# First rows of a one-core encoder layer: where S5's exponential, the mixing weights' row sums, the row scaling and the third weights' products stand in the order of work

## The chip, the cores and the metric

The kernel runs on one core of a Trainium2 chip. Its engines work side by side, each through its own queue in order: TensorE (PE; its weight loads PEld are shown apart), VectorE (DVE), ScalarE (ACT), GpSimd (POOL) and SyncE (SP), which issues most of the loads. The metric is the device time of one execution in microseconds, lower is better. Three runs of the kernel before took 872.94, 875.28 and 876.23 us; their median is 875.28 us.

## The reference

One encoder layer over 512 rows of width 1024, batch 1, in float32, cut to what matters here:

```python
def rms_norm(x, g):
    xf = x.astype(jnp.float32)
    y = xf * lax.rsqrt(jnp.mean(xf * xf, axis=-1, keepdims=True) + EPS)
    return (y * g.astype(jnp.float32)).astype(x.dtype)
...
    n = rms_norm(h, mix_norm_g[i])
    proj = n @ w_in[i]
    xa = proj[..., :OFF_U]
    zu = proj[..., OFF_U:OFF_V]
    zv = proj[..., OFF_V:OFF_GA]
...
    step = jnp.exp(log_step.astype(f32))[:, None]
    lam_bar = jnp.exp(lam * step)
```

Behind that come an S5 branch (two linear recurrences over the rows), a gated branch that mixes rows with weights `sgu_w`, a merge of both, cross-attention to 256 memory rows, and a SwiGLU block. The change lies wholly in the start: the norm of x, the first columns of `n @ w_in`, and the first steps of S5's and the mixing branch's setup.

## The kernel before

Every matrix product is made of three TensorE products: both operands are split into a rounded part ("hi", a cast on ScalarE) and its rest ("lo", a subtraction on VectorE), and `mm3` (L390) adds hi x hi, hi x lo and lo x hi. A weight tile is loaded as `wraw` (SP's queue, three buffers), then split to `whi` and `wlo` by `split` (L83). `plan` (L99) lists all weight tiles in the order in which they are used, and `next_w` (L365) issues loads three tiles ahead and splits two ahead. The final order on each engine is set by a scheduler, which may move instructions as data allow; `in_order` holds an instruction at its place in the program, and so does `pinned` for what `split` issues.

The rows are handled in four tiles of 128. A tile is normalized, turned (transposed to features by rows on TensorE, eight 128x128 transposes in two halves, `to_feat`, L548, tile `ptr`), and the turned half is split into `xn` hi and lo by ScalarE and VectorE. `first_rows` (L607) does this for row tile 0, with g broadcast by a product with ones (`pg`, L611), two idle products (`idles`, L586), and the first weights split in halves of 512 columns between the turned halves. The loop at L629 does row tiles 1 to 3: the row sums of squares on ScalarE (`row_sums`, L531), the factor (`rms_factor`, L519: two small VectorE operations and a power on GpSimd), the scaling (L541), the turning. Here "row 1" means row tile 1, and "second turning" the turning of row tile 1.

The first products are `tokm(w_in, OFF_V, ...)` (L1095): token-major, one bank `pt` of 512 columns for each row tile, over four weight tiles of 256 features each. The first two weight tiles are multiplied tile by tile; the last two ("third" and "fourth weights") are held and multiplied row tile by row tile. A row tile and a weight tile make six 128x512 products. Behind it come two feature-major blocks (`pf`), for S5's input.

Beside this runs `s5_setup` (L673), a generator whose steps the scheduler places among the products: the loads of the step sizes (`ls`, L684), of lambda (`lrows`, L688, turned to `plam`, L690), of b (`brow`, L700, turned to `pbc`, L705), of d (`dcol`, L811) and c (`crow`, L713), and the exponential of the step sizes (L726). `row_weights` (L1133) sums the mixing weights `wsx` over their last axis (L1136), a reduction on VectorE; their load is at L1126.

Of the kernel before, what the change touches and what calls it, by code (L numbers as in the profile page):

```python
# [2 lines left out]

# [6 lines left out]
F32 = mybir.dt.float32  # L10
F32R = mybir.dt.float32r
AF = mybir.ActivationFunctionType
ALU = mybir.AluOpType
AX = mybir.AxisListType
# [6 lines left out]
NT = T // P  # L21
KD = D // P
# [13 lines left out]
OFF_V = OFF_U + GW  # L36
# [16 lines left out]
def hybrid_layer_kernel(  # L53
# [8 lines left out]
    nc = tc.nc  # L62
    x, mem, out = x[0], mem[0], out[0]
    w_in, w_glu, w_proj_a, w_proj_b, w_out = w_in[0], s5_w_glu[0], w_proj_a[0], w_proj_b[0], w_out[0]
# [12 lines left out]
    def bank(name):  # L77
        return pm.tile([P, 512], F32, tag="mm", name=name)

    def aux(name, shape=(P, 512)):  # L80
        return pa.tile(list(shape), F32, tag="aux", name=name)

    def split(dst_hi, dst_lo, src):  # L83

        hi = nc.scalar.copy(dst_hi, src)  # L85
        lo = nc.vector.tensor_tensor(dst_lo, src, dst_hi.bitcast(F32), ALU.subtract)  # L86
        if pinned[0]:
            in_order(hi)
            in_order(lo)


    pinned = [False]
    in_order = tc.keep_in_program_order


# [64 lines left out]
    stp = [None]  # L160
# [226 lines left out]
    def split_w(j):  # L387
        tiles.append(plan[j][2]())
# [40 lines left out]

    RATE = 0.8  # L430

    def tokm(w, c0, act, nk, evac, ntok=NT, last=2, kpt=2, hook=None, cut=None, t0=0):

        toks = range(t0, t0 + ntok)
        ps = {t: bank(f"pt{t - t0}") for t in toks}
        nw = nk // kpt
        held = []
        full = slice(0, 512)
        for wi in range(nw):
            hi, lo = next_w(w, wi * kpt, kpt, c0, 512)  # L440
            held.append((wi, hi, lo))
            if hook is not None and wi == nw - last:
                hook()
            if wi < nw - last:
                todo, held = held, []
                for t in toks:
                    end = cut is not None and t == ntok - 1 and wi == nw - last - 1
                    tok_block(ps[t], t, todo, act, kpt, full, wi == 0, end)
                    if end:
                        cut(None, ps[t])  # L450
                tick(1.3 * ntok)
        for t in toks:
            if cut is not None and t == ntok - 1:
                for i in range(2):
                    p = aux("pcut", (P, 256))
                    tok_block(p, t, held, act, kpt, slice(256 * i, 256 * i + 256), True, True)
                    cut(i, p)
            else:
                tok_block(ps[t], t, held, act, kpt, full, nw == last, True)
                evac(t, ps[t])  # L460
            tick(1.3 * len(held))

    def tok_block(ps, t, ws, act, kpt, cs, first, final):
        tsl = slice(t * P, (t + 1) * P)
        for i, (wi, hi, lo) in enumerate(ws):
            for k in range(kpt):
                kk = wi * kpt + k
                mm3(ps, (act[0](kk, tsl), act[1](kk, tsl)) if callable(act[0]) else
                    (act[0][:, kk, tsl], act[1][:, kk, tsl]),
                    (hi[:, k, cs], lo[:, k, cs]), first and i == k == 0,  # L470
                    final and i == len(ws) - 1 and k == kpt - 1)
# [47 lines left out]
    def rms_factor(ss, r=None):  # L519

        ms = np_.tile([P, 1], F32, tag="ms", name="ms", bufs=2)
        if r is None:
            r = np_.tile([P, 1], F32, tag="r", name="r", bufs=2)
        nc.vector.tensor_tensor(ms, ss[:, 0:1], ss[:, 1:2], ALU.add)
        nc.vector.tensor_scalar(ms, ms, 1.0 / D, EPS, ALU.mult, ALU.add)
        nc.gpsimd.tensor_tensor(r, ms, mhalf, ALU.pow)
        return r

    HALF = (slice(0, 512), slice(512, 1024))
# [7 lines left out]
    def rms_scale(src, g, dst, ss=None):  # L537

        r = rms_factor(row_sums(src) if ss is None else ss)
        for i in range(2):  # L540
            nc.vector.scalar_tensor_tensor(dst[:, HALF[i]], src[:, HALF[i]], r, g[:, HALF[i]], ALU.mult, ALU.mult)  # L541
# [6 lines left out]
    def to_feat(src, hi, lo, tsl, full=None, skip=None, part=(0, 1), behind=None):  # L548

        for q in part:  # L550
            ps = aux("ptr", (P, 4, P))
            for j in range(4):
                k = 4 * q + j
                tr = nc.tensor.transpose(ps[:, j, :], src[:, k * P:(k + 1) * P], ident)  # L554
                if behind is not None:
                    in_order(tr)
            if q != skip:
                split(hi[:, 4 * q:4 * q + 4, tsl], lo[:, 4 * q:4 * q + 4, tsl], ps)
            if full is not None:
                nc.scalar.copy(full[:, 4 * q:4 * q + 4, tsl], ps)  # L560
        if behind is not None:
            long_idle(behind)
# [23 lines left out]
    def idles(n):  # L586
        for i in range(n):
            in_order(nc.tensor.matmul(idle, ones, ones, start=True, stop=True))
# [6 lines left out]
    g_mix = np_.tile([P, D], F32, tag="gain", name="g_mix", bufs=2)  # L595
    g_row = np_.tile([1, D], F32, tag="gain", name="g_row", bufs=2)
    nc.sync.dma_start(g_row, mix_norm_g)
    xt = slot("A", (P, NT, D), F32, "xt")
# [6 lines left out]
    xn = (xn_hi, xn_lo)  # L605

    def first_rows():  # L607

        pg = [aux("pg") for i in range(2)]
        for i in range(2):  # L610
            in_order(nc.tensor.matmul(pg[i], ones[0:1, :], g_row[:, HALF[i]], start=True, stop=True))  # L611
        idles(2)
        r = rms_factor(row_sums(xt[:, 0, :]))
        for i in range(2):
            in_order(nc.scalar.copy(g_mix[:, HALF[i]], pg[i]))
            in_order(nc.vector.scalar_tensor_tensor(xt[:, 0, HALF[i]], xt[:, 0, HALF[i]], r, pg[i], ALU.mult, ALU.mult))
        raw = plan[0][3].pop("raw")
        hi = wp.tile([P, 2, 512], F32R, tag="hi", name="whi", bufs=3)
        lo = wp.tile([P, 2, 512], F32R, tag="lo", name="wlo", bufs=3)
        pinned[0] = True  # L620
        for q in range(2):
            split(hi[:, q, :], lo[:, q, :], raw[:, q, :])
            to_feat(xt[:, 0, :], xn_hi, xn_lo, slice(0, P), part=(q,))
        tiles.append((hi, lo))

    first_rows()
    split_w(1)
    ss = row_sums(xt[:, 1, :])
    for t in range(1, NT):  # L629
        rms_scale(xt[:, t, :], g_mix, xt[:, t, :], ss)  # L630
        if t == 1:
            ss = row_sums(xt[:, 2, :])
        to_feat(xt[:, t, :], xn_hi, xn_lo, slice(t * P, (t + 1) * P))
        if t == 1:
            ss3 = row_sums(xt[:, 3, :])
            pinned[0] = False
        if t == 2:
            ss = ss3

# [31 lines left out]
    def s5_setup():  # L673
        A_ = nc.scalar
# [3 lines left out]
        def small():  # L678
            used[0] += 1
            return slab[:, used[0] - 1, :]  # L680

        ls = small()
        for d in range(2):
            nc.sync.dma_start(ls[64 * d:64 * d + 64, :], s5_log_step[0, d].partition_broadcast(64))  # L684
        lam = []
        lrows = s5p.tile([G, 2, 2, 64], F32, tag="etmp", name="lrows")
        for i, src in enumerate((s5_lam_re, s5_lam_im)):
            nc.sync.dma_start(lrows[:, i], src[0].rearrange("d g p -> g d p"))  # L688
            ps = aux("plam", (P, G))
# [12 lines left out]
        for q in range(2):  # L702
            ps = aux("pbc", (P, C // 2, 2, G))
# [10 lines left out]
        for i in range(2):  # L714
            ps = aux("pbc", (P, G * C // P, P))
# [6 lines left out]
        st["c"] = (cr, ci)  # L722


        stp, a, rho, th, n, sn, hs, cs = (small() for _ in range(8))
        A_.activation(stp, ls, AF.Exp)  # L726
        V.tensor_tensor(a, lr, stp, ALU.mult)
        A_.activation(rho, a, AF.Exp)
        V.tensor_tensor(th, li, stp, ALU.mult)
# [11 lines left out]
        t0, t1 = small(), small()  # L741
# [52 lines left out]
        w = s5p.tile([P, 2, G, C], F32, tag="etmp", name="bbw")  # L794
# [289 lines left out]
    def zv_evac(half):  # L1084
        def f(t, ps):
            nc.scalar.activation(zt[:, t, half * 512:(half + 1) * 512], ps, AF.Gelu_apprx_tanh,
                                 accum_out=zsum[:, t, half:half + 1])
        return f
# [3 lines left out]
    wsr, wst = wsx[:, 0], wsx[:, 1]  # L1092
    side["gen"] = s5_program()
    side["rate"] = RATE
    tokm(w_in, OFF_V, xn, KD, zv_evac(0))  # L1095

    u = s5p.tile([P, G, NCH], F32, tag="u", name="u")

# [34 lines left out]
    def row_weights():  # L1133

        rs = np_.tile([P, 2 * H], F32, tag="gbc", name="rs", bufs=1)[:, 0:H]
        nc.vector.tensor_reduce(rs, wsr, AX.X, ALU.add)  # L1136
        later(0.5, lambda: turn_sums(rs))

    def turn_sums(rs):
# [42 lines left out]
    for h in range(H):  # L1182
        ps = bank("psv")
# [421 lines left out]
    full = fp.tile([P, KD, T], F32, tag="full", name="full", bufs=1)  # L1605
# [3 lines left out]
    held = []  # L1609
    for t0 in (0, 2):  # L1610
        ps = {t: bank(f"pt{t - t0}") for t in (t0, t0 + 1)}
# [77 lines left out]
    ps = [bank("pf0"), bank("pf1")]  # L1689
# [65 lines left out]
    for i, u in enumerate(UNITS):  # L1755
        final = i == len(UNITS) - 1
        x, v = begun
        q = unit_bank("pq")
# [111 lines left out]
    held = []  # L1870
# [50 lines left out]
```

## Time and profile before

| | |
|---|---|
| median of three runs | 875.28 us (872.94 to 876.23) |
| profiled execution | 875.6 us |
| its span, first to last instruction | 873.8 us |
| TensorE busy | 860.3 us, 98% |
| VectorE busy | 648.0 us, 74% |
| ScalarE busy | 475.6 us, 54% |
| GpSimd busy | 108.8 us, 12% |
| mean granted TensorE clock | 0.991 |

A row of the timeline reads: start, duration (both us), engine, line of the kernel, operation, what it writes and reads, and in brackets how long the engine stood idle before it and who released it. SPq is SP's queue, and its rows are the issues of transfers. A row of the windows reads: stretch and its length, then for each engine the busy time and the number of instructions in it, the granted clock of TensorE (1.00 is full speed), the busy share of the DMA engines and GB/s. A row of the chain of waits reads: start, duration, what the end of the program was waiting for then.

### The profile page before, as it was taken

The numbers are of one execution on the slowest core, as the hardware profiler recorded it, in microseconds if no ns is written. First come the engines' busy times: TensorE is split into PE (matmuls) and PEld (weight loads), VectorE is DVE, ScalarE is ACT, GpSimd is POOL, SyncE is SP. The second block draws the span as 40 slices with busy tenths as digits, with TensorE's granted clock in tenths as the row PEclk, the third lists the DMA queues.
The fourth block names the chain that finished last, engine by engine and source line by source line (L and its number), as shares of the span: only waits on it lengthen the run. The fifth ranks groups of instructions, "written<-read, shape, count | busy, mean of one in ns | idle before, by whom it ended". The sixth has DMA issues, their size and how long they took to land.

```text
span 873.8 us, 14852 instructions
## 1 busy us (share of the span) xinstructions
PE 860.3 (98%) x5897; PEld 764.8 (88%) x5897; DVE 648.0 (74%) x897; ACT 475.6 (54%) x704; POOL 108.8 (12%) x157
## 2 busy tenths in 40 slices
PE   8999999999999999999999999999999999999996
PEld 6788888878889988889899878999999999888875
DVE  5599679867748768679658656867877778889875
ACT  5453875267436544557547444645545454655663
POOL 1000066100611010110000001001111111000000
PEclk8999999999999999999999999999999999999998
DMA  7457559844647687934688144557799777467672
GB/s 235 121 154 223 115 179 234 203 121 153 173 121 197 162 223 202 287 113 167 204 253 218 54 151 110 145 135 177 173 222 228 201 194 167 135 205 229 197 249 85
DMA packets 110119, 155.40 MB, mean 178 GB/s; under 512 B 8969, under 2 KB 77089, under 8 KB 109986
## 3 DMA queue, kind: packets, MB, share of 16 engines
q1 hardware_dynamic: 91746, 128.27, 45.1%
q0 software_dynamic: 18016, 25.66, 18.5%
q8 instruction: 46, 0.75, 0.3%
q10 hardware_dynamic: 288, 0.52, 0.2%
q14 instruction: 23, 0.19, 0.1%
HBM read 148.70 MB, written 37.20 MB: 213 GB/s over the span
## 4 chain that ended last, share of the span: by engine, by line
PE 95%; DVE 1%; DMA 1%; SPq 1%; ACT 0%; issue 0%; POOLq 0%; POOL 0%; ACTq 0%
PE pf L393 27%; PE pt L393 18%; PE px L1221 12%; PE dx L393 7%; PE pq L1221 6%; PE dq L393 3%; PE pv L1221 3%; PE gx L1221 3%; PE qx L1221 2%; PE dv L393 2%; PE py L1015 1%; DMA slab<-in_s_log_step_dram 1%; PE gq L1221 1%; PE ptr L554 1%; PE po L393 1%; PE qq L1221 1%
## 5 line engine op out<-in xcount | busy, mean ns | idle before, releaser
L86 DVE TENSOR_TENSOR wlo<-wraw,whi 128x1024 fp32r<-128x1024 f32 (+1 forms) x135 | 160.0, 1185 | 82.4 <-ACT whi L85 82.0
L85 ACT CAST whi<-wraw 128x1024 fp32r<-128x1024 f32 (+1 forms) x135 | 138.0, 1023 | 145.0 <-PE pf L393 46.9
L393 PE MATMUL pf<-xn,whi 128*128 128x512 f32 x320 | 100.4, 393 | 0.0
L1221 PE MATMUL px<-fn,whi 128*128 128x256 f32 x480 | 83.3, 276 | 0.0
L1221 PEld LDWEIGHTS px<-fn,whi 128*128 128x128 f32 x480 | 72.5, 188 | 0.3 <-ACT u L1776 0.2
L393 PEld LDWEIGHTS pf<-xn,whi 128*128 128x128 f32 x320 | 59.5, 188 | 12.7 <-issue 0.7
L86 DVE TENSOR_TENSOR wlo<-b,whi 128x1024 fp32r<-128x1024 f32 x40 | 48.9, 1222 | 28.9 <-ACT whi L85 28.9
L85 ACT CAST whi<-b 128x1024 fp32r<-128x1024 f32 x40 | 42.2, 1054 | 51.2 <-PE px L1221 27.1
L1221 PE MATMUL px<-fn,wlo 128*128 128x256 f32 x240 | 66.4, 277 | 0.0
L393 PE MATMUL pf<-xn,wlo 128*128 128x512 f32 x160 | 62.6, 392 | 0.0
L393 PE MATMUL dx<-whi,s 128*128 128x512 f32 x170 | 53.9, 392 | 1.4 <-ACT whi L85 1.0
L1221 PE MATMUL pq<-s,whi 128*128 128x256 f32 x320 | 55.1, 276 | 0.0
L86 DVE TENSOR_TENSOR wlo<-t,whi 128x1024 fp32r<-128x1024 f32 x30 | 36.7, 1224 | 19.9 <-ACT whi L85 19.9
L85 ACT CAST whi<-t 128x1024 fp32r<-128x1024 f32 x30 | 31.6, 1053 | 35.8 <-PE pv L1221 12.6
L1221 PEld LDWEIGHTS pq<-s,whi 128*128 128x128 f32 x320 | 48.3, 188 | 0.1
L393 PE MATMUL pt<-whi,xn 128*128 128x512 f32 x128 | 45.4, 430 | 1.9 <-ACT xn L85 1.9
L1221 PEld LDWEIGHTS px<-fn,wlo 128*128 128x128 f32 x240 | 45.1, 188 | 0.0
L1221 PE MATMUL pq<-s,wlo 128*128 128x256 f32 x160 | 44.2, 277 | 0.0
L393 PEld LDWEIGHTS dx<-whi,s 128*128 128x128 f32 x170 | 31.7, 188 | 8.5 <-ACT whi L85 1.2
L393 PEld LDWEIGHTS pf<-xn,wlo 128*128 128x128 f32 x160 | 30.1, 188 | 6.3 <-issue 0.2
L311 POOL DMA_DIRECT2D dsum<-in_w_down_dram x12 | 13.3, 1108 | 163.3 <-DMA dsum<-in_w_down_dram 163.3
L393 PE MATMUL dx<-wlo,s 128*128 128x512 f32 x85 | 33.1, 390 | 0.0
(478 smaller groups left out, 2342.4 us busy)
## 6 DMA issues: line engine op xcount, KB each, us to landing
wraw<-in_w_in_dram SPq DMA_DIRECT2D x35, 512.0 KB, 5.4
dsum<-in_w_down_dram SPq DMA_DIRECT2D x20, 512.0 KB, 5.7
wraw<-dsum SPq DMA_DIRECT2D x20, 512.0 KB, 3.9
b<-in_w_gate_dram SPq DMA_DIRECT2D x15, 512.0 KB, 4.8
b<-in_w_up_dram SPq DMA_DIRECT2D x15, 512.0 KB, 4.5
wraw<-in_w_down_dram SPq DMA_DIRECT2D x15, 512.0 KB, 4.0
dsum<-in_w_down_dram POOLq DMA_DIRECT2D x10, 512.0 KB, 7.7
dsum<-dsum POOLq DMA_DIRECT2D x10, 512.0 KB, 5.5
```

Of the source, the lines that this page charges most:

```text
L85: hi = nc.scalar.copy(dst_hi, src)
L86: lo = nc.vector.tensor_tensor(dst_lo, src, dst_hi.bitcast(F32), ALU.subtract)
L311: plan[j + step][1].append((0, lambda d=dst, x=more: nc.gpsimd.dma_start(d, x, accum_op=ALU.add)))
L393: nc.tensor.matmul(ps, a[x], b[y], start=start and i == 0, stop=stop and i == 2, skip_group_check=free)
L554: tr = nc.tensor.transpose(ps[:, j, :], src[:, k * P:(k + 1) * P], ident)
L1015: in_order(nc.tensor.matmul(ps[64 * j:64 * j + 64, :], a, b, start=g % 4 == k == 0, stop=k == 2, tile_position=(0, 64 * j), skip_group_che ...
L1221: nc.tensor.matmul(ps[:, j, :], a[x], b[y], start=start and j == k == i == 0, stop=k == 3 and i == 2, skip_group_check=True)
```

## The change

Six edits. In `first_rows` the two idle products are gone, and row 0's scaling is issued ahead of the copies of g. The first weights' split is written out, with each half of g's copy between the cast of that half and the turned rows, and the subtraction behind the turned rows. In the loop, the scaling of row tiles 1 to 3 is placed behind the last subtraction of the turning before (`tc.issue_after`). The split of the third weights is placed behind row 1's scaling. The products of the third and fourth weights with row tile 0 are placed behind row 1's last transpose (`behind`, passed to `tokm`). The exponential of the step sizes and the mixing weights' row sums are placed behind the cast and the subtraction of the last turned rows. `issue_after` sets a place in the order; it computes nothing.

```diff
@@ split
         if pinned[0]:
             in_order(hi)
             in_order(lo)
+        return hi, lo
...
-    pinned = [False]
+    pinned, turned, row_tr = [False], [], [None]
@@ tokm
-    def tokm(w, c0, act, nk, evac, ntok=NT, last=2, kpt=2, hook=None, cut=None, t0=0):
+    def tokm(w, c0, act, nk, evac, ntok=NT, last=2, kpt=2, hook=None, cut=None, t0=0, behind=None):
...
-                tok_block(ps[t], t, held, act, kpt, full, nw == last, True)
+                with nullcontext() if behind is None or t > t0 else tc.issue_after(behind):
+                    tok_block(ps[t], t, held, act, kpt, full, nw == last, True)
@@ to_feat
                 tr = nc.tensor.transpose(ps[:, j, :], src[:, k * P:(k + 1) * P], ident)
+                row_tr[0] = tr.ins
...
-                split(hi[:, 4 * q:4 * q + 4, tsl], lo[:, 4 * q:4 * q + 4, tsl], ps)
+                turned[:] = split(hi[:, 4 * q:4 * q + 4, tsl], lo[:, 4 * q:4 * q + 4, tsl], ps)
@@ first_rows
-        idles(2)
         r = rms_factor(row_sums(xt[:, 0, :]))
-        for i in range(2):
-            in_order(nc.scalar.copy(g_mix[:, HALF[i]], pg[i]))
-            in_order(nc.vector.scalar_tensor_tensor(xt[:, 0, HALF[i]], xt[:, 0, HALF[i]], r, pg[i], ALU.mult, ALU.mult))
...
         pinned[0] = True
+        for i in range(2):
+            in_order(nc.vector.scalar_tensor_tensor(xt[:, 0, HALF[i]], xt[:, 0, HALF[i]], r, pg[i], ALU.mult, ALU.mult))
         for q in range(2):
-            split(hi[:, q, :], lo[:, q, :], raw[:, q, :])
+            in_order(nc.scalar.copy(hi[:, q, :], raw[:, q, :]))
+            in_order(nc.scalar.copy(g_mix[:, HALF[q]], pg[q]))
             to_feat(xt[:, 0, :], xn_hi, xn_lo, slice(0, P), part=(q,))
+            in_order(nc.vector.tensor_tensor(lo[:, q, :], raw[:, q, :], hi[:, q, :].bitcast(F32), ALU.subtract))
@@ the loop over row tiles 1 to 3
-        rms_scale(xt[:, t, :], g_mix, xt[:, t, :], ss)
+        r = rms_factor(ss)
+        with tc.issue_after(turned[1].ins):
+            for i in range(2):
+                scaled = nc.vector.scalar_tensor_tensor(xt[:, t, HALF[i]], xt[:, t, HALF[i]], r, g_mix[:, HALF[i]], ALU.mult, ALU.mult)
...
             pinned[0] = False
+            with tc.issue_after(scaled.ins):
+                split_w(2)
+            turned1 = row_tr[0]
...
+    last_row = [x.ins for x in turned]
@@ s5_setup
             nc.sync.dma_start(ls[64 * d:64 * d + 64, :], s5_log_step[0, d].partition_broadcast(64))
+        stp = small()
+        with tc.issue_after(last_row[0]):
+            A_.activation(stp, ls, AF.Exp)
...
-        stp, a, rho, th, n, sn, hs, cs = (small() for _ in range(8))
-        A_.activation(stp, ls, AF.Exp)
+        a, rho, th, n, sn, hs, cs = (small() for _ in range(7))
@@ the first products
-    tokm(w_in, OFF_V, xn, KD, zv_evac(0))
+    tokm(w_in, OFF_V, xn, KD, zv_evac(0), behind=turned1)
@@ row_weights
-        nc.vector.tensor_reduce(rs, wsr, AX.X, ALU.add)
+        with tc.issue_after(last_row[1]):
+            nc.vector.tensor_reduce(rs, wsr, AX.X, ALU.add)
```

The scheduler's order follows from it, engine by engine. TensorE: all six products of the third weights with row 0 stand behind row 1's transposes (before, one of them stood ahead); row 2's eight transposes stand behind all 18 products of row 1 and ahead of row 2's, row 3's eight behind all 18 of row 2 (before, row 2's eight and row 3's first four stood together, and row 3's last four two products later). ScalarE: cast of the first weights' first half, copy of g's first half, cast of the turned first half, and the same for the second. VectorE: the first weights' rests each behind the rest of a turned half. SP: the fourth weights' load behind S5's fourth d load, the mixing weights and the first of the gated branch's gains; the seventh weights' load ahead of S5's four c loads. Behind some 300 us the order is the same on every engine.

2 lines of the change are left out of this document (1 added, 1 removed).

## The prediction

> **What bounds the kernel now.** I read the page first, then the chain of waits, then the busy time over the long middle, and last the timeline of the first 40 us, where the change lies.
>
> ```profile
> span 873.8 us, 14852 instructions
> ...
> PE 95%; DVE 1%; DMA 1%; SPq 1%; ACT 0%; issue 0%; POOLq 0%; POOL 0%; ACTq 0%
> ```
>
> ```profile
> 45.00:866.00 821.00, 818.17 (x5724) 732.70 (x5723) 620.49 (x823) 448.27 (x647) 103.73 (x142) 1.00 0.65 178
> ```
>
> ```profile
> 5.97 11.27 DMA slab<-in_s_log_step_dram
> 18.09 7.15 PE pt L393 x23
> ...
> 46.87 21.59 PE pf L393 x95
> ```
>
> From 45 to 866 us TensorE is busy 818.17 of 821 us at full clock (1.00 in the column of the granted clock), so whatever TensorE gains ahead of 45 us arrives at the end undiminished, and nothing behind 45 us can be gained by this change. The one piece of the chain that is not TensorE is a load: S5's step sizes, which take 11.27 us from 5.97 on to land. A product (a 128x512 matmul) steps at 21.59 / 95 = 0.227 us at full clock.
>
> The first rows, in order of time:
>
> ```profile
> 6.75 0.59 ACT L615 COPY g_mix<-pg 128x512 f32<-128x512 f32 x1 [1.44 <-PE pg L611]
> 7.44 1.53 DVE L616 SCALAR_TENSOR_TENSOR xt<-xt,r,pg 128x512 f32<-128x512 f32 x2 [1.75 <-ACT g_mix L615]
> 7.50 0.71 PE L588 MATMUL idle<-ones 128*128 128x128 f32 x4
> 7.60 0.59 ACT L615 COPY g_mix<-pg 128x512 f32<-128x512 f32 x1 [0.27 <-PE pg L611]
> 8.09 0.62 ACT L85 CAST whi<-wraw 128x512 fp32r<-128x512 f32 x1
> 8.33 1.81 PE L554 MATMUL ptr<-ident,xt 128*128 128x128 f32 x8
> 8.99 0.59 ACT L85 CAST xn<-ptr 128x512 fp32r<-128x512 f32 x1 [0.28 <-PE ptr L554]
> 10.66 1.05 ACT L85 CAST whi<-wraw 128x1024 fp32r<-128x1024 f32 x1
> 11.74 1.23 DVE L86 TENSOR_TENSOR wlo<-wraw,whi 128x1024 fp32r<-128x1024 f32 x1 [0.24 <-ACT whi L85]
> 13.99 1.41 DVE L541 SCALAR_TENSOR_TENSOR xt<-xt,r,g_mix 128x512 f32<-128x512 f32 x2 [0.67 <-POOL r L526]
> 14.79 1.38 PE L554 MATMUL ptr<-ident,xt 128*128 128x128 f32 x8
> 15.32 1.22 DVE L86 TENSOR_TENSOR wlo<-wraw,whi 128x1024 fp32r<-128x1024 f32 x1
> 17.33 0.23 ACT L726 ACTIVATE slab<-slab 128x32 f32<-128x32 f32 x1 [1.82 <-DMA slab<-in_s_log_step_dram]
> 17.47 1.06 ACT L85 CAST xn<-ptr 128x512 fp32r<-128x512 f32 x2
> 18.09 0.50 PE L393 MATMUL pt<-whi,xn 128*128 128x512 f32 x1 [1.91 <-ACT xn L85]
> ```
>
> The second turning (transposes at 14.79) is finished at 16.17, but ScalarE stands in the exponential, which waits for that load, and casts the turned rows only at 17.47. TensorE stands for 1.91 us.
>
> The stall has a second price, in the clock. Products alone (L393), cut at the moments at which the granted clock changes and at the same distance between them:
>
> ```profile
> 8.90:12.32 3.42, 2.53 (x6) 2.12 (x7) 0.50 1.05 370
> 12.32:15.73 3.41, 2.33 (x8) 1.11 (x7) 1.00 0.91 160
> 15.73:19.14 3.41, 1.05 (x5) 0.88 (x6) 1.00 0.36 55
> 19.14:22.55 3.41, 3.41 (x10) 2.67 (x9) 0.50 1.00 293
> ...
> 32.79:36.21 3.42, 1.63 (x5) 0.48 (x3) 1.00 0.00 0
> 36.21:39.62 3.41, 3.14 (x7) 2.48 (x8) 0.50 0.55 123
> ```
>
> The clock is 1.00 or 0.50 for periods of 3.41 us. After a period with 1.05 or 1.63 us of products comes half clock, after one with 2.33 or 2.53 us full clock. Where TensorE is the bound, such a period loses half of 3.41, or 1.7 us. Two of them (from 19.14 and from 36.21) lie in reach of the change; the one from 8.90 lies where VectorE sets the pace.
>
> **The change part by part.**
>
> *Scaling ahead of g's copy, and the new order of the first rows.* Scaling no longer stands behind the copy. The copy's start shows g's broadcast ready at 6.75, so scaling starts at 6.75 instead of 7.44, the transposes at 7.64 instead of 8.33, and their cast could start at 7.64 + (8.99 - 8.33) = 8.30. But ScalarE's queue now holds the first weights' cast and g's copy ahead of it, and the cast waits for its load:
>
> ```profile
> L137 SPq DMA_DIRECT2D wraw<-in_w_in_dram x5: 395/434/826, 1.6 to 19.5; - x5
> ...
> DMA to landing us min/median/max: 5.8/6.0/6.2
> ```
>
> Issued at 1.6, it lands at 7.4 to 7.8. I take 7.8. ScalarE's half tiles step at 8.09 - 7.60 = 0.49, so the turned rows' cast is at 7.8 + 2 x 0.49 = 8.78, only 0.21 earlier, and the second weights' cast at 7.8 + 6 x 0.49 = 10.74 instead of 10.66. VectorE now subtracts the second turned half (from 10.87) and the second half of the first weights ahead of the second weights' rest; a half is 0.61, half of the 1.23 row, so that rest starts at 12.10 instead of 11.74. Row 1's sums are read behind it, so row 1's scaling starts at 14.35 and its transposes at 15.15: 0.36 later. Bounds: 0.69 earlier (the whole lead kept) to 0.7 later. The two idle products less cost nothing: they ran at 7.50, while the transposes waited for the scaling.
>
> *The exponential behind the last rows, the third weights behind the second turning.* With the exponential gone from ScalarE's queue, the cast of the turned rows 1 starts at 15.15 + 0.66 = 15.81. The transposes end at 15.15 + 1.38 = 16.53; the third weights' first product follows at once, having been moved from before them. The second waits for VectorE: scaling 14.35 + 1.33, then the third weights' rest 1.22, so 16.90, and 16.96 at TensorE. That is what is late next. At 16.96 there are 5 products of the third weights and 18 of row 1 left, the 23 of the chain's row at 18.09. So 1.13 us earlier, the 0.36 included. Bounds: 0 (VectorE later by as much) and 1.9 (the whole stall).
>
> *Mixing sums behind the last rows, rows 2 and 3 apart.*
>
> ```profile
> 23.81 1.22 DVE L1136 TENSOR_REDUCE rs<-wsx 128x8 f32<-128x1024 f32 x1 [2.47 <-DMA wsx<-in_sgu_w_dram]
> ...
> 25.07 1.48 PE L554 MATMUL ptr<-ident,xt 128*128 128x128 f32 x12
> 26.35 0.50 PE L393 MATMUL pt<-whi,xn 128*128 128x512 f32 x1
> 27.08 0.66 PE L554 MATMUL ptr<-ident,xt 128*128 128x128 f32 x4
> 27.49 0.70 PE L393 MATMUL pt<-whi,xn 128*128 128x512 f32 x2
> 30.87 0.24 PE L690 MATMUL plam<-ident,lrows 32*128 32x32 f32 x1
> 33.94 1.10 PE L705 MATMUL pbc<-ident,brow 64*128 64x64 f32 x8
> 35.41 1.14 PE L705 MATMUL pbc<-ident,brow 64*128 64x64 f32 x8
> ```
>
> The sums waited 2.47 us for their weights, with row 3's scaling behind them on VectorE. TensorE paid little: rows 2 and 3 were turned together, 16 transposes (1.28 / 12 = 0.107 each, 1.71) and two products (0.46) in 27.49 - 25.07 = 2.42, so 0.25 idle. The changed order turns row 2 behind all of row 1's products, then multiplies it, then turns row 3. Each turning stands alone: 1.28 to its first product, of which 0.86 is transposes; the third product waits for VectorE's rest of the turned half and follows about 0.8 behind the first, after 0.46 of products. That is 0.42 + 0.34 = 0.76 idle a row, 1.27 more than before for both. S5's two small transposes (0.24) and some of the waits around S5's b rows fall into row 3's gaps instead of standing by themselves, together about 0.7. I take 0.55 later; bounds 0 and 1.3. Row 3's scaling is no longer the bound.
>
> At the new place the reduction (1.22) stands ahead of the fourth weights' rest on VectorE:
>
> ```profile
> 17.53 0.40 SPq L137 DMA_DIRECT2D wraw<-in_w_in_dram  x1
> ...
> 19.01 0.42 SPq L1128 DMA_DIRECT2D gbr<-in_sgu_ln_g_dram  x1
> ...
> 33.21 1.05 ACT L85 CAST whi<-wraw 128x1024 fp32r<-128x1024 f32 x1 [1.39 <-PE pt L393]
> ```
>
> The fourth weights' cast waits for row 3's first block of products, and VectorE needs that cast; the reduction runs in this wait, with the exponential on ScalarE. Without that cover each would cost its own length, 1.22 and 0.23. On SP's queue the fourth weights' load goes behind S5's last d load, the mixing weights and the first gain: issued near 19.0 instead of 17.53, landed by 19.0 + 6.2 = 25.2. It is needed when row 3's first block is multiplied: row 2 is turned at 16.96 + 23 x 0.227 = 22.2, its products and the turning of row 3 take 22.2 + 5.7 + 2.1 = 30.0, the block ends near 31. Some 6 us of cover: nothing. The seventh load now stands ahead of S5's four c loads; it waits for the fourth weights' rest (31.1 + 1.05 + 1.23 = 33.4), they wait for the b transposes, which end about 1 us later: nothing.
>
> *The clock.* Without a spell in between, the products of the fourth weights start near 36 us. The stretch without products at the second turning shrinks from 3.3 us (14.79 to 18.09) to about 2.0 (the last product before it starts near 14.4, four steps behind the second weights' rest at 13.46; the next is at 16.53): a period that holds it whole has some 1.4 us of products, one that is cut by it over 2.4. The b transposes now have eight products between them; row 3's turning with the first eight leaves about 1.7 us of products in the worst period. Both lie about where the rows (1.63 half, 2.33 full) leave it open, and how the periods fall decides. I take one spell of the two away: 1.7 us. Bounds: both away (3.4), or a third one, for row 2 (1.7 the other way).
>
> The sum, against the profiled execution (875.6 us, of which 1.8 lie around the span): 1.13 - 0.55 + 1.7 = 2.3 us less, 873.3 us. That execution is 0.3 above the median of the runs shown (875.28), which I leave in the range.
>
> **The rivals.**
>
> *Both spells go.* For it: every product-free stretch in the new order is 2 us or shorter. Against it: the period from 32.79 had 1.63 us of products and was still followed by half clock. 875.6 - 0.58 - 3.4 = 871.6 us. The Trainium skill (TensorE: Matmul & The Clock Gate, part 1, what is actually happening, and the table of why it matters) states that half clock follows at least one idle window of about 3.4 us, and advises against gaps above 3 us. By that rule this rival would win; the trace agrees with the length of the period (3.41), but shows half clock after a period with 1.05 us of products in it.
>
> *The wait is handed on, and the clock keeps both spells.* VectorE takes ScalarE's place at the second turning, or the stretch of 2.0 us is enough. For it: VectorE is the next late engine by only 0.4 us, and ScalarE's cast of the first weights may wait longer for its load. Then only 0.58 us or nothing is left: 875.0 us (873.9 to 875.9). Here the change does not do what it says.
>
> *Slower: row 2 gets a spell of its own.* Turned alone, row 2 has 1.6 us without products inside 2.1, so a period around it has some 1.8 us of products. If half clock follows anything under 2.0 us, then second turning, row 2 and row 3 each bring one: three instead of two. 875.6 - 0.58 + 1.7 = 876.7 us. Against it: the period from 12.32, with 2.33 us, was followed by full clock, and three periods would all have to fall badly.
>
> **How the numbers follow.** Forecast, one spell away: 0.40 (873.3; its own range 872.2 to 874.4). Both away: 0.26. None away or handed on: 0.24. Slower by row 2: 0.10. The range reaches from the lower half of the second case to the middle of the last: 870.9 to 876.5. A measurement of this kernel can tell about 0.5%, or 4.4 us, from no change. Faster than 870.9 takes both spells and most of the upper bounds: 0.17, from the second case. Slower than 879.7 needs a cost that no case prices: 0.06. The rest, 0.77, is no difference that can be told.
>
> **What would show it.** Right: the turned rows' cast near 15.8 with no exponential ahead of it; TensorE's idle at the second turning below 0.6 us, ended by VectorE; rows 2 and 3 turned in two groups of eight with 0.4 and 0.3 us idle behind each; full clock in one of the two periods; fourth weights' products between 36 and 38 us instead of 40. Wrong: a stall behind the second turning still above 1.5 us; the first turned cast later than 9.0; idle time at a load of the fourth weights; or a difference that arises behind 45 us.

## The result and the profile after

The changed kernel takes 876.72 us (median of 22 executions, 873.95 to 878.84), the kernel before 874.69 us in the same session (22 executions, 872.80 to 876.23): a ratio of 1.0023 with a 95% interval of 1.0013 to 1.0032. The change costs about 2 us; the forecast was a gain of 2.3.

The page of the changed kernel, its span and the chain of waits by engine:

```profile
span 876.3 us, 14843 instructions
...
PE 94%; DVE 2%; ACT 2%; issue 1%; DMA 1%; SPq 0%; POOL 0%; POOLq 0%; DVEq 0%; ACTq 0%
```

TensorE's share of the chain fell from 95 to 94%, VectorE's and ScalarE's rose to 2% each: the end now also waits for splits. Where, two late rows of the chain show when they are held against the same rows of before (start, duration, line, number of products). First the kernel before, then the changed one; `psv` is the first mixing product, `pt` x75 a stage behind all gates:

```profile
154.00 7.14 PE psv L1185 x64
...
338.44 17.00 PE pt L393 x75
```

```profile
152.10 7.14 PE psv L1198 x64
...
340.92 17.01 PE pt L394 x75
```

At `psv` the changed kernel is 1.90 us ahead, at `pt` 2.48 us behind, and so it stays: 876.3 - 873.8 = 2.5 at the end. Between the two marks it needs 188.82 us where the kernel before needs 184.44. In these two executions the start did gain, and 4.38 us are lost in a stretch where the prediction expected nothing. The windows say where (busy time of PE, PEld, DVE, ACT and POOL, then the granted clock, the DMA share and GB/s), before and after:

```profile
185.00:225.00 40.00, 39.98 (x360) 32.30 (x359) 26.13 (x31) 29.71 (x31) 5.51 (x15) 1.00 0.53 142
...
274.00:282.00 8.00, 8.00 (x71) 8.00 (x70) 5.17 (x7) 5.96 (x8) 1.20 (x1) 1.00 0.79 192
```

```profile
185.00:225.00 40.00, 39.38 (x357) 31.70 (x356) 25.29 (x30) 29.60 (x31) 6.46 (x19) 1.00 0.55 147
...
274.00:282.00 8.00, 6.14 (x39) 6.07 (x39) 6.57 (x7) 3.62 (x5) 2.02 (x2) 0.79 0.88 132
```

In eight microseconds of the gate stage TensorE issues 39 products where it issued 71, stands 1.86 us, and its clock is 0.79. The changed kernel's list of waits (who waits for whom, total, times, longest) names two places, a row of TensorE the first of them, and a narrow window the half clock:

```profile
PE gx L1234 <- DVE wlo L86: 1.9, 1, 1.9
...
PE pk L876 <- POOL bd L852: 0.6, 1, 0.6
```

```profile
275.94 0.39 PE L1234 MATMUL gx<-gse,wlo 128*128 128x256 f32 x1 [1.85 <-DVE wlo L86]
```

```profile
276.40:279.70 3.30, 3.30 (x18) 3.30 (x17) 3.30 (x4) 0.00 (x0) 1.35 (x1) 0.51 0.94 157
```

So the gate stage loses 1.85 us to a wait for VectorE and 1.6 us to the 3.3 us at 0.51 directly behind it, 3.5 of the 4.38. Another 0.6 us is lost at the S5 products `pk`, at 221 us and so ahead of the gate stage; the rest has no row. A wait at `pk` comes and goes: of the kernels below that have the gate stage in its old order, g36_exp stands 0.66 us between 185 and 225 us and g36 not at all.

Why VectorE is late there is seen on ScalarE's and VectorE's timelines of 255 to 276 us. The kernel before, ScalarE:

```profile
259.77 1.04 ACT L85 CAST gsd<-x 128x1024 fp32r<-128x1024 f32 x1 [1.90 <-PE pf L393]
260.73 1.04 ACT L85 CAST whi<-gw 128x1024 fp32r<-128x1024 f32 x1
...
264.86 0.60 ACT L1023 ACTIVATE tt<-py 128x512 f32<-128x512 f32 x1 [1.65 <-PE py L1015]
```

The changed kernel, ScalarE and then VectorE:

```profile
262.30 0.60 ACT L1035 ACTIVATE tt<-py 128x512 f32<-128x512 f32 x1 [5.74 <-PE py L1027]
262.79 1.13 ACT L85 CAST yg<-ygt 128x512 fp32r<-128x512 f32 x2
263.82 0.60 ACT L1035 ACTIVATE tt<-py 128x512 f32<-128x512 f32 x1
264.31 1.05 ACT L85 CAST gsd<-x 128x1024 fp32r<-128x1024 f32 x1
265.25 1.06 ACT L85 CAST whi<-gw 128x1024 fp32r<-128x1024 f32 x1
```

```profile
263.44 1.30 DVE L86 TENSOR_TENSOR yg<-ygt,yg 128x512 fp32r<-128x512 f32 x2 [8.10 <-ACT yg L85]
265.39 1.22 DVE L86 TENSOR_TENSOR gsd<-x,gsd 128x1024 fp32r<-128x1024 f32 x1 [0.66 <-ACT gsd L85]
```

Before, the casts of the gates' first sum (`gsd`) and of the third gate weights (`gw`) run at 259.77, and the Gelu of S5's second outputs behind them. After, that Gelu stands ahead of them in ScalarE's queue and waits 5.74 us for its products; the casts behind it start at 264.31, and VectorE, which has the rests of `yg` first, idles 8.10 us. The backlog reaches TensorE ten microseconds later. None of these lines is touched by the change: the scheduler ordered them anew (why it did is not shown).

The start itself went as forecast in its order. TensorE of the changed kernel (the row at 25.91 is row 2's third product):

```profile
5.62 3.78 PE L614 MATMUL pg<-g_row,ones 1*128 1x512 f32 x4
...
17.32 1.04 PE L556 MATMUL ptr<-ident,xt 128*128 128x128 f32 x8
18.11 0.47 PE L394 MATMUL pt<-whi,xn 128*128 128x512 f32 x1
...
23.91 1.04 PE L556 MATMUL ptr<-ident,xt 128*128 128x128 f32 x8
25.18 0.50 PE L394 MATMUL pt<-whi,xn 128*128 128x512 f32 x1 [0.24 <-ACT xn L85]
...
25.91 0.73 PE L394 MATMUL pt<-whi,xn 128*128 128x512 f32 x2
...
29.66 1.04 PE L556 MATMUL ptr<-ident,xt 128*128 128x128 f32 x8
```

The stall behind the second turning is gone, and rows 2 and 3 are turned in two groups of eight. The first product of row 2 starts 1.27 us after its first transpose, the third 0.73 us after the first. This execution is some 2 us late from the first broadcast on, which took 3.78 us against 1.98 in the profile of before.

### The profile page after: what moved, and what is told of

Its sections match the earlier page's. It is cut to its first block, busy times and chain, and to the rows that moved or that the text cites. A ratio compares the mean times of both kernels' runs of the same rounds, so it can differ in the third digit from the quotient of the medians.

```text
span 876.3 us, 14843 instructions
## 1 busy us (share of the span) xinstructions
PE 862.0 (98%) x5893; PEld 764.9 (87%) x5893; DVE 647.7 (74%) x897; ACT 474.8 (54%) x704; POOL 106.1 (12%) x157
## 4 chain that ended last, share of the span: by engine, by line
PE 94%; DVE 2%; ACT 2%; issue 1%; DMA 1%; SPq 0%; POOL 0%; POOLq 0%; DVEq 0%; ACTq 0%
PE pf L394 24%; PE pt L394 18%; PE px L1234 12%; PE dx L394 7%; PE pq L1234 6%; PE dq L394 3%; PE pv L1234 3%; PE qx L1234 2%; PE gx L1234 2%; PE dv L394 2%; PE ptr L556 1%; PE po L394 1%; PE qq L1234 1%; PE py L1027 1%; DMA gw<-in_w_in_dram 1%
```

## The experiments on the gate stage

**g36, b36.** One number, on the changed kernel and, as a control, on the kernel before:

```diff
-        while side["now"] < 34:
+        while side["now"] < 36:
             yield None
         yield from s5_outputs(1)
```

> The changed kernel with one number altered: S5's second outputs are released from step 36 of the side program instead of 34, which puts the casts of the gates' operands and weights ahead of the Gelu of S5's second outputs again on ScalarE, as in the kernel before; nothing ahead of 250 us is different from the changed kernel. Theory (the order of the gate stage takes the gain back: 1.86 us of idle TensorE and some 1.7 us of half clock between 274 and 282 us): the idle time there goes, the time falls by 3.5 us from 876.7 to about 873.2 us (872.5 to 873.9), and lies below the kernel before. Rival (the start of the changed kernel or the chance of a half-clock period costs it, and the gate stage is only where a profile happened to show it): 876 to 877 us.

> Control: the same number altered in the kernel before. Its casts already stand ahead of that Gelu, and one cast and one small product change places. Theory (the order of the gate stage takes the gain back): as the kernel before, 874.7 us (874.2 to 875.2). Rival (the later release is a gain by itself, whatever the start): 1 us or more less, 873.7 or below.

g36 takes 872.43 us, ratio to the kernel before 0.9977 (0.9963 to 0.9991); b36 takes 874.19 us, 1.0003 (0.9988 to 1.0017). ScalarE and a window of g36:

```profile
255.66 1.04 ACT L85 CAST gsd<-x 128x1024 fp32r<-128x1024 f32 x1 [1.91 <-PE pf L394]
256.62 1.04 ACT L85 CAST whi<-gw 128x1024 fp32r<-128x1024 f32 x1
...
260.84 0.60 ACT L1035 ACTIVATE tt<-py 128x512 f32<-128x512 f32 x1 [1.75 <-PE py L1027]
```

```profile
274.00:282.00 8.00, 8.00 (x69) 8.00 (x69) 6.15 (x7) 4.90 (x7) 1.20 (x1) 1.00 0.77 153
```

The casts are ahead of the Gelu again, TensorE is busy throughout at full clock, and the kernel lies 4.3 us below the changed one (4.0 by the two ratios, since the sessions differ) and 0.23% below the kernel before. The number alone does nothing that can be told to the kernel before. The theory holds: the order of the gate stage, not the start, makes the change slower.

**b_held.** The kernel before, with its start untouched and the casts held back by hand:

```diff
-                nc.scalar.activation(y, ps.rearrange(...), AF.Gelu_apprx_tanh)
+                st["sq"] = nc.scalar.activation(y, ps.rearrange(...), AF.Gelu_apprx_tanh).ins
...
-                ops = halves(b11 if q in (1, 7) else t)
+                with tc.issue_after(st["sq"]) if (q, i) == (5, 0) else nullcontext():
+                    ops = halves(b11 if q in (1, 7) else t)
...
-    split(*gops[5], gsum[1])
-    split(*gops[6], gsum[2])
+    with tc.issue_after(st["sq"]):
+        split(*gops[5], gsum[1])
+        split(*gops[6], gsum[2])
```

> The kernel before, its start untouched, with the casts of the gates' first sums and of the third gate weights held behind the Gelu of S5's second outputs, as the changed kernel's order has them. Theory (that order costs an idle TensorE at the gate products and the half clock behind it): 2 to 3.8 us more than the kernel before, 876.7 to 878.5 us. Rival (TensorE has other products to go on with, and the order costs nothing): 874.7 us (874.2 to 875.2).

878.97 us, ratio 1.0053 (1.0034 to 1.0073), from 7 executions: 4.8 us more, above the range of the theory. VectorE and TensorE of b_held:

```profile
263.13 1.29 DVE L86 TENSOR_TENSOR yg<-ygt,yg 128x512 fp32r<-128x512 f32 x2 [9.35 <-ACT yg L85]
```

```profile
276.12 0.38 PE L1222 MATMUL gx<-gse,wlo 128*128 128x256 f32 x1 [2.16 <-DVE wlo L86]
```

The same wait at the same product. The order alone, with the old start, makes the loss. It isn't an exact copy of the changed kernel's order: on ScalarE one copy of `part` stays ahead of the Gelu and the cast of the second gate sum (`gse`) comes ahead of that of the weights, and some groups of products change places on TensorE. Its profile has no half clock in the gate stage, so the loss does not need one; its idle time between 185 and 282 us is 3.2 us, and the rest of its loss has no row.

The stretch from `psv` to `pt`, held against all profiles, says the same: 188.82 us in the changed kernel, 188.68 in b_held, and between 183.86 and 184.77 in the other fifteen, whatever their start.

## The experiments on the start

With the gate stage in order the start's gain reaches the end, and its parts can be priced.

**Parts taken out of g36.** In g36_exp the exponential stands where it stood before; in g36_third the third weights are neither split nor multiplied behind anything; in g36_first the first rows are in the old order, with their idle products.

> As g36, but S5's exponential stands where the kernel before has it, ahead of row 1's turned cast on ScalarE; all other engines keep their order. Theory (the exponential's wait for its load stops TensorE behind the second turning, and the gain of the first stage reaches the end once the gate stage is in order): 1.1 us more than g36 by the stall and up to 1.7 more where a half-clock period follows it, so 1.1 to 2.8 us above g36. Rival (the third weights' rest on VectorE is late by as much, so the exponential's place is worth nothing): within 0.4 us of g36.

> As g36, but the third weights are split and multiplied without being held behind row 1's scaling and turning, as in the kernel before; rows 2 and 3 are still turned apart, and only products of the first rows change places. Theory (the start's gain comes from the clock, and the stretches without products are what counts): within 0.5 us of g36, 872.0 to 872.9 us, as the place of five products shortens no such stretch. Rival (the third weights' place is what ends the stall at the second turning): about 1 us more than g36, 873.4 us or above.

> As g36, but row 0 is scaled, turned and cast in the order of the kernel before, with its two idle products: copies of g ahead of the scaling and of the first weights' cast. Theory (the first rows' new order costs as much as it gains, since ScalarE's queue waits for the first weights' load): within 0.4 us of g36, 872.0 to 872.8 us. Rival (the earlier scaling is the gain of the start): 0.7 to 1.7 us more than g36, 873.1 to 874.1 us.

872.66 us (0.9983, 0.9969 to 0.9998), 872.51 us (0.9975, 0.9960 to 0.9989) and 871.04 us (0.9957, 0.9943 to 0.9972). Taking out the exponential or the third weights' place costs nothing that can be told. (In the profile of g36_exp the step sizes' load landed early, and the exponential waited 0.29 us for it.) The old first rows looked 1.4 us better, outside both expectations, so they were run again below.

**b_warm.** Six idle products directly behind the second turning of the kernel before, to ask whether the gain is the clock:

```diff
         to_feat(xt[:, t, :], xn_hi, xn_lo, slice(t * P, (t + 1) * P))
+        if t in (1,):
+            with tc.issue_after(row_tr[0]):
+                for _ in range(6):
+                    nc.tensor.matmul(idle, ones, ones, start=True, stop=True)
```

> The kernel before with six idle products (128x128, some 0.18 us each at full clock) put on TensorE directly behind the second turning, where it stands for 0.6 to 1.9 us; no other instruction changes place. Theory (what the new start gains is mostly fewer half-clock periods, since three executions of other kernels with either start reach the first mixing product at 150.6 to 150.9 us where no such period falls on the products): the stretch without products behind the second turning is filled, and the median falls by half to all of one such period, 0.8 to 1.7 us, to 872.5 to 873.4 us. Rival (the gain is the work itself, in time that TensorE waits): the idle products stand ahead of the next ones, and the time is unchanged to 0.5 us longer, 874.2 to 874.7 us.

875.02 us, 1.0001 (0.9987 to 1.0015). Filling that one stretch gains nothing that can be told. The wait for the mixing weights, a second stretch without products, is left in this kernel. Its profiled execution is at full clock from 6 us to the end of the start and takes 876.91 us all the same: the broadcast of g took 3.78 us in it, and from `pt` to its end it needs 2.3 us more than the kernel before (537.6 against 535.4). So executions differ by more than the clock of the start.

**b_sums.** The kernel before with the mixing sums alone behind the last rows:

> The kernel before with one instruction moved: the reduction of the mixing weights stands behind the rests of row 3's turned halves on VectorE instead of ahead of row 3's scaling; every other instruction keeps its place. Theory (TensorE paid 0.25 us for that wait, and rows 2 and 3 stay together): 874.2 us less 0 to 0.3. Rival (the wait of 2.47 us for the mixing weights was a price of the start, also through the clock): 1 us or more less, 873.2 us or below.

874.19 us, 0.9992 (0.9974 to 1.0009): nothing that can be told, as the theory said, though not for its reason. In the profile the exponential's wait is still there, and half clock follows it (a row of TensorE, then a window):

```profile
17.67 0.63 PE L394 MATMUL pt<-whi,xn 128*128 128x512 f32 x1 [1.61 <-ACT xn L85]
```

```profile
18.00:21.10 3.10, 3.10 (x9) 2.33 (x9) 2.56 (x7) 1.34 (x5) 0.58 (x2) 0.50 0.83 197
```

**g36_copy, gf_joint, gf_rows, gf_again.** In g36_copy each copy of g stands ahead of the first weights' cast:

```diff
         for q in range(2):
-            in_order(nc.scalar.copy(hi[:, q, :], raw[:, q, :]))
             in_order(nc.scalar.copy(g_mix[:, HALF[q]], pg[q]))
+            in_order(nc.scalar.copy(hi[:, q, :], raw[:, q, :]))
```

The other three have g36_first as their base: gf_joint without the hold on the rows' scaling, gf_rows with exponential and third weights in their old places, gf_again the same kernel once more.

> As g36, but on ScalarE each copy of a half of g stands ahead of the cast of the first weights' half instead of behind it; scaling stays ahead of both. Theory (the new order of the first rows costs, because row 0's second four transposes wait 0.49 us for the copy that frees their bank, and the copy stands behind a cast that waits 2.22 us for its load): those transposes start near 8.3 us instead of 9.03, the second turning near 14.6 instead of 15.27, and the time is 0.7 to 1.7 us less than g36, 870.7 to 871.7 us. Rival (the first rows' order costs nothing by itself, and g36_first was lower by its two idle products or by chance): 872.0 to 872.9 us, as g36.

> As g36_first, but the scaling of rows 1 to 3 is not held behind the rest of a turned half, so that TensorE's order of the first rows is that of the kernel before (rows 2 and 3 turned together, 16 transposes and two products), while exponential, mixing sums and third weights stay where the change puts them. Theory (what the start gains comes from rows 2 and 3 being turned apart, which this study had booked as 0.55 us of loss): 1 to 3 us more than g36_first, 872.2 to 874.2 us. Rival (the exponential's and the third weights' places carry it together, though each alone was worth 0.2 us or less): 870.6 to 871.6 us.

> The other way round: as g36_first, but exponential and third weights stand as in the kernel before; mixing sums and the scaling of the rows stay as changed, so rows 2 and 3 are turned apart. Theory (rows 2 and 3 apart): within 0.5 us of g36_first, 870.6 to 871.6 us. Rival (exponential and third weights together): 1 us or more above it, 872.0 us or more.

> g36_first once more, as the measure for the three beside it. If its lead of 1.4 us over g36 is the first rows' order: 870.6 to 871.6 us. If it was the chance of how half-clock periods fell: about 872.4 us.

872.24 us (0.9975, 0.9961 to 0.9990), 871.88 us (0.9980, 0.9965 to 0.9995), 872.99 us (0.9984, 0.9967 to 1.0000) and 872.34 us (0.9978, 0.9962 to 0.9994). gf_again is g36_first once more, and its ratio is 0.0021 higher: most of g36_first's lead was chance, and no price of the first rows' order is shown. It also says how far two sessions of one kernel can lie apart: by as much as the whole gain of the start. What follows therefore rests on groups of kernels, not on one ratio. Rows 2 and 3 turned apart carry nothing either: gf_joint turns them together. In g36 row 0's second four transposes do wait for g's copy, and in g36_copy they don't (TensorE of g36, then of g36_copy), but the second turning starts no earlier:

```profile
7.51 1.03 PE L556 MATMUL ptr<-ident,xt 128*128 128x128 f32 x4 [0.55 <-DVE xt L621]
9.03 1.12 PE L556 MATMUL ptr<-ident,xt 128*128 128x128 f32 x4 [0.49 <-ACT g_mix L624]
...
15.27 1.20 PE L556 MATMUL ptr<-ident,xt 128*128 128x128 f32 x8
16.94 0.50 PE L394 MATMUL pt<-wlo,xn 128*128 128x512 f32 x1 [0.25 <-DVE wlo L86]
```

```profile
7.59 1.84 PE L556 MATMUL ptr<-ident,xt 128*128 128x128 f32 x8 [0.32 <-DVE xt L621]
...
15.38 1.03 PE L556 MATMUL ptr<-ident,xt 128*128 128x128 f32 x8
```

**b_exp, b_expthird, b_expred.** The kernel before with the exponential alone moved, then with one more move:

```diff
             nc.sync.dma_start(ls[64 * d:64 * d + 64, :], s5_log_step[0, d].partition_broadcast(64))
+        stp = small()
+        with tc.issue_after(last_row[0]):
+            A_.activation(stp, ls, AF.Exp)
...
-        stp, a, rho, th, n, sn, hs, cs = (small() for _ in range(8))
-        A_.activation(stp, ls, AF.Exp)
+        a, rho, th, n, sn, hs, cs = (small() for _ in range(7))
```

b_expred has besides it only this:

```diff
-        nc.vector.tensor_reduce(rs, wsr, AX.X, ALU.add)
+        with tc.issue_after(last_row[1]):
+            nc.vector.tensor_reduce(rs, wsr, AX.X, ALU.add)
```

> The kernel before with one instruction moved: S5's exponential stands behind the casts of the last rows on ScalarE instead of ahead of row 1's turned cast. Theory of the prediction (TensorE stands 1.91 us because ScalarE waits there for the step sizes' load; the load lands between 14.9 and 17.3 us in the profiles seen since, so the stall is there in some executions and not in others): half of the 1.13 to 1.9 us on the median, 0.5 to 1.5 us less than the kernel before. Rival (the exponential's place is worth nothing, as taking it out of g36 cost 0.2 us): within 0.4 us of the kernel before.

> As b_exp, and one product of the third weights stands behind the second turning instead of ahead of it. Theory (exponential's stall, and a product that fills the time behind the turning): 0.2 to 0.5 us less than b_exp. Rival (that product hides nothing): as b_exp within 0.4 us.

> As b_exp, and the mixing sums stand behind the last rows on VectorE (both moves behind the last rows, without the rest of the change). Theory (the two waits for loads in the first 30 us are what the start gains): 1.5 to 2 us less than the kernel before, as g36. Rival (each and both are worth nothing, and the gain lies in the first rows' order or behind 45 us): within 0.5 us of the kernel before.

875.53 us, 1.0002 (0.9987 to 1.0017); 875.26 us, 1.0003 (0.9992 to 1.0013); 873.56 us, 0.9978 (0.9966 to 0.9990). By its ratio b_exp lies where its rival said, though the interval reaches 1.1 us down. b_expthird cannot be told from b_exp, so no effect of its one product is shown. b_expred meets its theory by the ratio (1.9 us less; 1.4 by the medians). The kernels with the gate stage in order fall into three groups that don't overlap:

| stands behind the last rows | kernels | ratio to the kernel before |
|---|---|---|
| neither, or the exponential alone | b36, b_warm, b_exp, b_expthird | 1.0001 to 1.0003 |
| the mixing sums alone | b_sums, g36_exp, gf_rows | 0.9983 to 0.9992 |
| both | g36, g36_third, g36_first, gf_again, g36_copy, gf_joint, b_expred | 0.9957 to 0.9980 |

The exponential alone gains nothing; the sums alone gain 0.1 to 0.2%, both some 0.25%. Neighbouring groups lie within the interval of a single ratio, so the order of the groups is shown and the size of each step is not. VectorE, TensorE and a window of b_exp say why:

```profile
23.91 1.22 DVE L1140 TENSOR_REDUCE rs<-wsx 128x8 f32<-128x1024 f32 x1 [4.22 <-DMA wsx<-in_sgu_w_dram]
25.05 1.41 DVE L542 SCALAR_TENSOR_TENSOR xt<-xt,r,g_mix 128x512 f32<-128x512 f32 x2
```

```profile
25.89 0.63 PE L555 MATMUL ptr<-ident,xt 128*128 128x128 f32 x4 [3.26 <-issue]
```

```profile
26.80:29.40 2.60, 2.60 (x10) 2.00 (x9) 1.97 (x4) 1.06 (x3) 0.00 (x0) 0.50 0.00 0
```

With the exponential's stall gone, everything comes earlier to the next wait for a load: the mixing sums now wait 4.22 us for their weights (2.47 before), row 3's scaling stands behind them, TensorE idles 3.26 us ahead of row 3's transposes (its row names no releaser, but they read what the scaling at 25.05 writes), and a period at half clock follows. b_expthird's profile has the same stop, 1.79 us long. It is there too where nothing was moved, when the step sizes' load lands early by itself (TensorE of b36, whose exponential waited only 0.62 us; in b_held the stop is 1.01 us):

```profile
23.41 0.63 PE L554 MATMUL ptr<-ident,xt 128*128 128x128 f32 x4 [0.77 <-PE ptr L554]
```

The other way round, with the sums moved and the exponential in its old place, the stall behind the second turning is left (TensorE of gf_rows):

```profile
17.38 0.50 PE L394 MATMUL pt<-whi,xn 128*128 128x512 f32 x1 [1.13 <-ACT xn L85]
```

In b_expred, TensorE and a window:

```profile
17.39 1.38 PE L555 MATMUL ptr<-ident,xt 128*128 128x128 f32 x8
24.10 1.48 PE L555 MATMUL ptr<-ident,xt 128*128 128x128 f32 x12
26.10 0.66 PE L555 MATMUL ptr<-ident,xt 128*128 128x128 f32 x4
```

```profile
15.00:45.00 30.00, 29.18 (x144) 22.72 (x145) 20.98 (x61) 18.45 (x40) 1.65 (x3) 1.00 0.54 157
```

No wait for a load stands in the way of a row, and the clock is full for all of 15 to 45 us. Two moved instructions give the gain of the change, as far as these runs can tell, without its loss: the gate stage of this kernel has the order of the kernel before.

## Why the prediction was wrong, step by step

**The step that failed** is the sentence on which the whole sum stood: that what TensorE gains ahead of 45 us "arrives at the end undiminished", because TensorE is busy 818.17 of 821 us behind it. That share holds for the order in which it was measured. The change moved the scheduler's order in the gate stage. Between the two marks 4.38 us went, of which 3.5 have their rows in the gate stage and 0.6 at `pk`. g36 gives the loss back, b_held makes it with the old start. The section on the change itself calls the order the same only behind some 300 us; the stretch from 45 to 300 us was given no term. The prediction named "a difference that arises behind 45 us" as a sign against it, but gave it no price and no rival.

**The gain of the start** was right in size and wrong in some of its parts, so the size is in part luck. 2.3 us were forecast; g36 stands 0.23% under the kernel before, 2.0 us (0.8 to 3.2). The forecast was added up from one execution that had both a late load and two periods at half clock, and that reached `psv` at 154.00 us. b36 and b_held, with the same start, reached it at 150.86 and 150.80 in their profiles, g36 at 150.59: in executions in which the loads land early and the clock stays full from the second turning on, there is next to nothing to gain.

- The exponential: 1.13 us were booked on it alone. Its place is right to about a tenth: row 1's transposes were forecast at 15.15 and the second product behind them at 16.96, with VectorE late by some 0.4; g36 has 15.27, 16.94 and 0.25. But it gains nothing by itself (b_exp, b_expthird): in both profiles the mixing sums' load is the next bound. The question "what is late next" was answered for the second turning and not for row 3, eight microseconds on.
- The mixing sums: their wait of 2.47 us was priced by what TensorE paid for it then, 0.25 us. It was cheap only because the exponential had made the rows late already: where the exponential is early or moved, TensorE stands 0.77 to 3.26 us for it (b36, b_held, b_expthird, b_exp). The first wait hides the second, so the exponential's place has a price only once the sums are out of the way; the sums alone were worth 0.1 to 0.2%.
- Rows 2 and 3 apart: the steps were right. From first transpose to first product 1.28 us were forecast and 1.27 measured on row 2, from first to third product 0.8 and 0.73; counted as in the prediction that is 0.68 us of the 0.76 forecast. But gf_joint, which turns them together, shows neither gain nor loss, so the 0.55 us booked for it is not borne out at the end.
- The first rows: ScalarE's wait for the first weights was forecast to end at 7.8; it ended at 7.73 in the changed kernel. That the second four transposes would wait for g's copy was missed, at 0.49 us, without a price at the end. So was the clock there: in the four profiles with the new first rows and a broadcast of 2 to 2.4 us (g36, g36_exp, g36_third, g36_copy) half clock lasts some 6.7 us, two periods (in g36 from 7.7 to 14.4), in the ten with the old first rows and such a broadcast 3.4 us. Whether the idle products that went or the new order does it was not tried, and no price of it shows at the end.
- The clock: "one spell of two" was taken from one execution. Of the six profiles with the mixing sums in their old place two have one period at half clock from 17 us on, one has two, three have none; of eleven with the sums moved one has one, b_sums. As an estimate that makes a gain of 1.7 x (4/6 - 1/11) = 1.0 us through the clock, but no run tells it apart from the time waited.

**The rivals.** "Slower by row 2" gave 876.7 us, and 876.72 was measured: the right number by a mechanism that isn't there, since the changed kernel runs row 2 at full clock. "Both spells go" is what the clock of the start did in all profiles that have the whole change there (the changed kernel, g36, g36_copy), yet g36's 2.0 us are short of the 4 us that it added up: the two periods that go had been counted as if every execution had them. "Handed on" was the right thought at the wrong place: in b_exp the wait is handed on to row 3, where the sums stand in its way.

## What to carry to other kernels

Where a scheduler orders the engines' queues, an edit of the first microseconds can change queues far behind it, and every difference of order there needs to be found and priced, above all a queue in which a waiting instruction now stands ahead of one that could run. Of two waits for loads in a row the first can hide the second: taking away the first alone showed nothing here, its gain was waited away at the next, so follow the earlier arrival until it meets one. And one profiled execution is one draw of load landings and clock periods: a term read from a single landing or a single period should enter a sum with the share of executions that have it.

## What the hardware showed besides

A period at half clock can follow a short stop. In the changed kernel it came behind 1.85 us of idle time (clock 0.51 from 276.4), in b_held none came behind 2.16 us. So the length of a stop alone did not decide it here. The Trainium skill (TensorE: Matmul & The Clock Gate, part 1, what is actually happening) puts half rate behind at least one idle window of about 3.4 us; the length of the period agrees, but no stop of that length precedes the one at 276.4, and here the measurement decides.

The broadcasts of g took 1.98 us in most profiles, 2.03 to 2.36 in four, and 3.78 in three (the changed kernel, b_warm, b_expred), with the clock column at 1.00 throughout. The load of S5's step sizes let the exponential start at 14.95 us in b_held, at 15.49 in b36 and at 17.33 in the profile of before, from the same place in the same queue.
